# A four-layer hybrid decoder trunk on one core: masks, small weights and zeroed rows of a layer move to a pool of their own that is filled one stage earlier

## The chip, the core and the metric

The kernel runs on one core of one Trainium2 chip. The metric is the device time of one execution in microseconds (us), lower is better. TensorE (PE) multiplies matrices into PSUM, VectorE (DVE) and ScalarE (ACT) do the elementwise work, GpSimd (POOL) only fills tiles with constants here, and SyncE (SP) issues every DMA. Each engine works through its own instructions strictly in order; where one waits, everything behind it on that engine waits too.

## The reference

The trunk has 272 positions (16 learned meta tokens in front of 256 tokens) of width 1024 and four layers. Layer *i* has one token mixer of three kinds in turn, then a dense SwiGLU feed-forward block (FFN) with inner width 2816:

```python
for i in range(DEPTH):                      # 4 layers: fox, gla, gdn, fox
    y = rmsnorm(h, norm_mix[i])
    mix = (fox_mixer, gla_mixer, gdn_mixer)[i % 3](y, ...)
    h = h + mix
    h = h + swiglu(rmsnorm(h, norm_ffn[i]), w_gate_up[i], w_down[i])
return h[:, N_META:]
```

Fox is softmax attention with a forget bias, 16 heads of 64; GLA is gated linear attention with four heads; GDN is a gated delta rule with eight heads of 128 in chunks, whose inner step is a triangular solve:

```python
b = cumsum(g)                               # per chunk and head
lower = (k*beta) @ k.T * exp(where(strict, b_t - b_s, -inf))
u, w = triangular_solve(eye + lower, [v*beta, k*beta*exp(b)])
o = (q @ k.T * exp(where(incl, b_t - b_s, -inf))) @ (u - w @ state) + (q*exp(b)) @ state
```

All arithmetic is float32 in the reference.

## The kernel before

**Layout.** The residual `h` lies transposed in SBUF as eight tiles of 128 channels by 272 positions. Every dense product is kept near float32 precision by splitting both operands into a high and a low part (`zh`/`zl`, `oh`/`ol`, `ah`/`al` for the three kinds of activations, `wh`/`wl` for weights), so that a block of 128 x 128 weights against 272 columns costs three matmuls: high by high, high by low, low by high. I call such three matmuls a **block**, and name it by its operand: a `zh` block belongs to an input projection, an `oh` block to the mixer's output projection, an `ah` block to the FFN's second product. Chunked mixers work in three position tiles of 96, 96 and 80 (`TILES`).

**Weights.** 420 units of 512 KB, each eight blocks, arrive through one DMA each (`w`, issued by SP in `make_unit`, line 553 on). ACT copies a unit to `wh`, DVE subtracts to get `wl`. There are three raw buffers and three buffers of split units: the load of unit *u* waits until DVE has split unit *u*-3, and the split of *u* waits until PE is done with *u*-3. I count units from 0 in the order of the program: Fox 0 to 40, its FFN 41 to 106, GLA 107 to 139 with its output projection in the last eight, its FFN 140 to 205, GDN 206 to 246, and so on.

**Order of the work.** Nothing is scheduled on the chip. A planner in Python (`Trunk.turn`, `step`, `Lane.slot`, `Trunk.load`) runs generators for each small chain, and keeps for each engine a model of when it will be free and when each tile will be ready; dense blocks are the filler between the steps of the chains. PE's order is the planner's, and DVE, ACT, POOL and SP are ordered by the times that it computed. A load enters the model through `Trunk.load` (it moves the planner's clock of SP and of the DMA on), so a load that is moved or dropped also changes, by small amounts, the times by which the planner decides what stands next to what.

**Layers and their pools.** `run` (line 1720 on) calls, for each layer, `fox`, `gla` or `gdn` and then `ffn`. Each of these opens its own SBUF pools and closes them at its end, so the pools of a mixer lie on addresses that the FFN in front of it used; what is written first into them has to wait until the FFN's last reader, PE's last `ah` matmuls, is done. At the start of a mixer these are:

- `fox`: a load of its mask (`fmask`), used when the attention scores leave PSUM.
- `gla`: loads of its masks (`gmask`), of a tile of ones with zeros at the chunk starts (`rst`, 576 KB), by which one scan restarts its running sum at each chunk, and of a small weight (`wa`). `rst` and `wa` are used when the gate is computed.
- `gdn` (lines 1283 to 1296): loads of half masks (`half`) and a triangular mask (`tri`), two DVE casts of `tri` to `mask`, a cast of the identity to `eye`, a load of `rst`, and two tiles that DVE fills with zeros (`bs`, `brs`; `rows_tile` multiplies a column by 0).

**The seam between a mixer and its FFN, or an FFN and the next mixer.** For each of the eight output tiles *k*, DVE adds the product to the residual (`h<-h,ps`), ACT scales it to `zh` and squares it into `nsq`, DVE makes `zl` and adds the square to `nacc`. PE can run the next input projection for tiles 0 to 6 while tile 7 is still in this chain. After tile 7 PE sums `nacc` over the channels (`nacc,con`), DVE takes that as `ms` and computes the inverse root `rs` (nine instructions named `rq`), without which no projection can leave PSUM.

**GDN inside.** From `rs` a chain leads over the gate (`be`, `ax`, `l1p`), one scan (`b<-rst,ax`, line 1324), `rr` and `rc` to the decay matrices `d`. Later comes the inverse of the chunks' triangular matrices: a long DVE chain, then the merges (`xm,l`, `ym,xt`, `xt,ym`), then one solve for each of eight heads (`vb,xt`, `vn,l`, `d,vn`), beside the last input projections for q and v with their convolutions (`xc`, `yc`) on DVE. Four solved heads make a group; a group's sum of squares goes through the same inverse root, is spread by PE (`nacc,sel`) and gives four of the eight `oh` tiles, so that `oh` blocks of the first group can fill the gaps of the last solves.

## Time and profile before

| | us |
|---|---|
| median of three runs (lowest, highest) | 1561.16 (1558.8, 1566.98) |
| the profiled execution: its own time | 1560.21 |
| its span, first to last instruction | 1558.4 |
| PE busy / PE weight loads busy | 1498.1 / 1453.9 |
| DVE busy / ACT busy / POOL busy | 1096.2 / 780.2 / 17.1 |
| mean granted TensorE clock | 0.981 of full speed |
| moved by DMA | 225.85 MB, mean 145 GB/s |

Times of the trace count from the start of the span; the 1.8 us between span and time lie around it. In the profile a row of the timeline gives start, duration, engine, line, operation, `out<-in`, and in brackets how long the engine was idle before it and what ended that. Line 404 is the helper that issues every matmul, line 245 the one that issues every DVE, ACT and POOL instruction, line 377 the one for loads, so work is told apart by the names of its tiles. In the rows by window each engine has its busy time and its count of instructions; the column after them is the granted TensorE clock as a share of full speed.

The last residual tile of each stage is added at: first Fox layer 200 us, its FFN 398, GLA 541, its FFN 746, GDN 991, its FFN 1191, last Fox layer 1369; the last FFN runs to the end.

### The profile page before, as it was taken

The page shows a single profiled execution, that of the slowest core. Times are in us where ns is not written, and L with a number is a line of the kernel's source. Part 1 is how long each engine was busy: PE and PEld are TensorE (multiplying, and loading weights), DVE is VectorE, ACT ScalarE, POOL GpSimd, SP SyncE. Part 2 cuts the span into 40 slices and gives each one's busy share as a digit, 9 for nine tenths or more (in the row PEclk, how much of TensorE's full clock was granted, in tenths as well). Part 3 has the DMA queues.
Part 4 walks back from the last instruction along what each step waited for, and adds up shares of the span by engine and source line. Part 5 has one row for each costly group of instructions (what it writes and reads, how often), then busy time and mean ns, then how long its engine had stood idle before and what let it go on. Part 6 is the DMA issues. An engine that isn't in the chain of part 4 may idle for free.

```text
span 1558.4 us, 29526 instructions
## 1 busy us (share of the span) xinstructions
PE 1498.1 (96%) x11985; PEld 1453.9 (93%) x11985; DVE 1096.2 (70%) x2159; ACT 780.2 (50%) x1417; POOL 17.1 (1%) x56
## 2 busy tenths in 40 slices
PE   8899999999999999999897998999999999999999
PEld 7788999999999999999886897999999888999999
DVE  7778676665896776655779667866656777786653
ACT  5556554444455544444564544544445555654442
POOL 0000000000000000000200000000000000000000
PEclk9999999999999999999898898999999999999999
DMA  5232455555433455555333111555555333455564
GB/s 191 91 114 95 151 183 171 175 177 177 152 109 98 147 176 176 176 176 176 111 115 103 42 52 57 163 187 173 172 182 172 108 102 117 136 188 187 183 200 138
DMA packets 63897, 225.85 MB, mean 145 GB/s; under 512 B 7256, under 2 KB 9664, under 8 KB 63760
## 3 DMA queue, kind: packets, MB, share of 16 engines
q1 hardware_dynamic: 63760, 223.96, 43.9%
q8 instruction: 94, 1.54, 0.4%
q14 instruction: 43, 0.35, 0.1%
HBM read 222.88 MB, written 1.05 MB: 144 GB/s over the span
## 4 chain that ended last, share of the span: by engine, by line
PE 78%; DVE 9%; ACT 6%; issue 5%; DMA 0%; SPq 0%; POOL 0%; DVEq 0%; ACTq 0%; POOLq 0%
PE ps L404 78%; DVE wl L245 2%; ACT pr L245 2%; ACT wh L245 2%; DVE rq L245 1%; DVE pr L245 1%; DVE sm L245 1%; PE ps L409 1%; ACT d L245 1%; ACT pts L245 0%; DVE ri L245 0%; DVE raw L245 0%; DMA h<-in_h_dram 0%; DVE tmp L245 0%; DVE l1p L245 0%
## 5 line engine op out<-in xcount | busy, mean ns | idle before, releaser
L404 PE MATMUL ps<-zh,wh 128*128 128x272 f32 (+1 forms) x2400 | 712.1, 297 | 11.6 <-ACT zh L245 9.2
L404 PE MATMUL ps<-zh,wl 128*128 128x272 f32 (+1 forms) x2400 | 695.5, 290 | 5.4 <-DVE wl L245 5.4
L404 PE MATMUL ps<-zl,wh 128*128 128x272 f32 (+1 forms) x2400 | 696.6, 290 | 0.0
L245 ACT ACTIVATE wh<-w 128x1024 fp32r<-128x1024 f32 x420 | 443.6, 1056 | 392.5 <-PE ps L404 195.3
L245 DVE TENSOR_TENSOR wl<-w,wh 128x1024 fp32r<-128x1024 f32 x420 | 512.1, 1221 | 164.0 <-ACT wh L245 163.9
L404 PEld LDWEIGHTS ps<-zh,wh 128*128 128x128 f32 x2400 | 458.2, 191 | 21.4 <-ACT zh L245 9.5
L404 PEld LDWEIGHTS ps<-zh,wl 128*128 128x128 f32 x2400 | 458.3, 191 | 8.9 <-DVE wl L245 7.2
L404 PEld LDWEIGHTS ps<-zl,wh 128*128 128x128 f32 x2400 | 457.8, 191 | 0.2
L404 PE MATMUL ps<-al,wh 128*128 128x272 f32 (+1 forms) x704 | 202.0, 287 | 0.0
L404 PE MATMUL ps<-ah,wl 128*128 128x272 f32 (+1 forms) x704 | 201.3, 286 | 0.0
L404 PE MATMUL ps<-ah,wh 128*128 128x272 f32 (+1 forms) x704 | 200.7, 285 | 0.0
L404 PEld LDWEIGHTS ps<-ah,wh 128*128 128x128 f32 x704 | 133.0, 189 | 0.0
L404 PEld LDWEIGHTS ps<-al,wh 128*128 128x128 f32 x704 | 132.4, 188 | 0.0
L404 PEld LDWEIGHTS ps<-ah,wl 128*128 128x128 f32 x704 | 132.2, 188 | 0.0
L245 DVE TENSOR_TENSOR al<-a,ah 128x272 fp32r<-128x272 f32 (+1 forms) x88 | 38.6, 438 | 64.9 <-ACT ah L245 64.8
L245 DVE TENSOR_TENSOR s<-t,rs 128x272 f32<-128x272 f32 (+1 forms) x88 | 38.5, 437 | 64.5 <-ACT t L245 64.5
L404 PE MATMUL ps<-oh,wh 128*128 128x272 f32 (+1 forms) x256 | 76.3, 298 | 1.6 <-ACT wh L245 1.2
L404 PE MATMUL ps<-oh,wl 128*128 128x272 f32 (+1 forms) x256 | 75.4, 294 | 0.9 <-DVE wl L245 0.9
L404 PE MATMUL ps<-ol,wh 128*128 128x272 f32 (+1 forms) x256 | 75.1, 293 | 0.0
L245 ACT ACTIVATE zh<-h,par 128x272 fp32r<-128x272 f32 x64 | 32.7, 519 | 71.4 <-DVE h L245 70.6
L245 ACT ACTIVATE ah<-a 128x272 fp32r<-128x272 f32 (+1 forms) x88 | 36.8, 418 | 62.6 <-DVE a L245 62.6
L245 ACT ACTIVATE pr<-sm,mn 96x192 f32<-96x192 f32 (+3 forms) x96 | 42.2, 441 | 26.6 <-DVE mn L245 26.5
(224 smaller groups left out, 1501.5 us busy)
## 6 DMA issues: line engine op xcount, KB each, us to landing
w<-in_w_dram SPq DMA_DIRECT2D x420, 512.0 KB, 3.3
h<-in_h_dram SPq DMA_DIRECT2D x4, 272.0 KB, 5.4
out_dram<-h SPq DMA_DIRECT2D x8, 128.0 KB, 2.8
rst<-in_rst_dram SPq DMA_DIRECT2D x1, 576.0 KB, 6.0
mask<-in_fmask_dram SPq DMA_DIRECT2D x2, 210.0 KB, 5.6
con<-in_con_dram SPq DMA_DIRECT2D x1, 207.5 KB
mask<-in_gmask_dram SPq DMA_DIRECT2D x1, 126.0 KB, 3.1
par<-in_par_dram SPq DMA_DIRECT2D x1, 87.5 KB, 3.2
```

The source lines that it names most:

```text
L245: r = f(*args, **kw)
L404: ins = self.nc.tensor.matmul(out, lhsT, rhs, start=start, stop=stop)
L409: ins = self.nc.tensor.transpose(out, in_, self.con("ident")[:n, :n])
```

## The change

A new function `ready` opens a pool of its own for the next layer's mask, small weight, casts and zeroed tiles, loads or computes them, and leaves them in `self.pre`. `run` calls it for the first layer before the loop, and for every further layer right after the mixer in front of it is done and before that layer's FFN; the pool of the layer just ended is closed first. The mixers take their tiles from `self.pre`. `tri` lands in one of the two buffers that also hold the squares of the norm (`nsq`). Two tiles of ones and zeros are no longer loaded: GLA's `rst` is filled by two POOL memsets, and GDN's scan is split into one for each position tile, with a broadcast column of ones in the place of `rst`.

```diff
+    def ready(self, kind, last):
+        cx = ExitStack()
+        pp = cx.enter_context(self.tc.tile_pool(name="pre" + kind, bufs=1))
+        v = self.v
+        if kind == "fox":
+            w = sum(t0 + n for t0, n in TILES)
+            mask = pp.tile([96, w], F32, tag="mask", name="mask")
+            self.load(mask, self.io["fmask"][:, (w if last else 0) : (2 * w if last else w)])
+            self.pre = mask
+        elif kind == "gla":
+            mask = pp.tile([96, 96 + 5 * 48], F32, tag="mask", name="mask")
+            self.load(mask, self.io["gmask"])
+            wa = pp.tile([16, 512], F32, tag="wa", name="wa")
+            self.load(wa, self.io["wa"])
+            self.pre = mask, wa
+        else:
+            half = pp.tile([96, 96], F32, tag="half", name="half")
+            self.load(half, self.io["dmask"][:, 96:192])
+            tri = self.zp.tile([128, T], F32, tag="nsq", name="tri", bufs=2)[:96, :96]
+            self.load(tri, self.io["dmask"][:, 0:96])
+            dmask = pp.tile([96, 176], F32R, tag="mask", name="mask")
+            v.tensor_copy(dmask[:, 0:96], tri)
+            v.tensor_copy(dmask[:, 96:176], tri[:, 0:80])
+            eye = pp.tile([96, 96], F32R, tag="eye", name="eye")
+            v.tensor_copy(eye, self.con("ident")[:96, :96])
+            bs = self.rows_tile(pp, "bs")
+            brs = self.rows_tile(pp, "brs", T, 128)
+            self.pre = half, dmask, eye, bs, brs
+        return cx
...
@@ gla
-            self.load(rst, self.io["rst"])
-            wa = cp.tile([16, 512], F32, tag="wa", name="wa")
-            self.load(wa, self.io["wa"])
+            g.memset(rst, 1.0)
+            g.memset(rst.rearrange("p (i c) -> p i c", c=96)[:, :, 0:1], 0.0)
...
@@ gdn
-            half_mask = gp.tile([96, 96], F32, tag="half", name="half")
-            self.load(half_mask, self.io["dmask"][:, 96:192])
...
+            half_mask, dmask, eye, bs, brs = self.pre
...
-                v.tensor_tensor_scan(b, rst, x, 0.0, ALU.mult, ALU.add)
+                one = self.con("strip")[:8, 142:143]
+                for t0, n in TILES:
+                    v.tensor_tensor_scan(b[:, t0 : t0 + n], one.to_broadcast([8, n]), x[:, t0 : t0 + n], 0.0, ALU.mult, ALU.add)
...
@@ run
+            pre = self.ready(self.layers[0][1][0], n == 1)
             for i, (li, (kind, j)) in enumerate(self.layers):
...
                 getattr(self, kind)(j, lo, f"g_ffn{li}")
+                pre.close()
+                if not last:
+                    pre = self.ready(self.layers[i + 1][1][0], i == n - 2)
                 self.ffn(lo, None if last else f"g_mix{self.layers[i + 1][0]}", last)
```

Three places show what moves; a row's `x2` means that it stands twice.

DVE before, at the seam from GLA's FFN to GDN (`wl` is the split of a weight unit, the rest as above):

```order
L245 TENSOR_TENSOR wl<-w,wh 128x1024 x2
L245 CAST mask<-tri 96x96
L245 CAST mask<-tri 96x80
L245 CAST eye<-con 96x96
L245 TENSOR_SCALAR bs<-con 128x272
L245 TENSOR_SCALAR brs<-con 128x272
L245 TENSOR_TENSOR h<-h,ps 128x272
L245 SCALAR_TENSOR_TENSOR zl<-h,par,zh 128x272
```

The same place after the change; the `h` is tile 7, the last of the seam:

```order
L245 TENSOR_TENSOR wl<-w,wh 128x1024 x2
L245 TENSOR_TENSOR h<-h,ps 128x272
L245 SCALAR_TENSOR_TENSOR zl<-h,par,zh 128x272
L245 TENSOR_TENSOR nacc<-nacc,nsq 128x272
L245 TENSOR_SCALAR nacc<-con 128x272
L245 TENSOR_TENSOR wl<-w,wh 128x1024
```

The five instructions in front of tile 7 are gone from there. On ACT, tile 7's `zh` and `nsq` also come one `wh` copy earlier, and on PE `nacc,con` comes after seven `zh` blocks where it came after nine.

DVE after the change at the seam from GLA to its FFN, 200 us earlier in the program; before, the two casts are not there and the rest is the same. The `h` in the second row is tile 6, the last one tile 7:

```order
L245 TENSOR_TENSOR wl<-w,wh 128x1024
L245 TENSOR_TENSOR h<-h,ps 128x272
L245 SCALAR_TENSOR_TENSOR zl<-h,par,zh 128x272
L245 TENSOR_TENSOR nacc<-nacc,nsq 128x272
L245 CAST mask<-tri 96x96
L245 CAST mask<-tri 96x80
L245 TENSOR_TENSOR wl<-w,wh 128x1024
L245 TENSOR_TENSOR h<-h,ps 128x272
```

The first `wl` is that of unit 140, the second that of unit 141. `eye`, `bs` and `brs` stand some 30 rows further ahead, in GLA's last steps, between an `ob` and the `ol` of head tile 5. On SP the load of `half` comes after unit 137 and that of `tri` after unit 143; before, both came after unit 210. The masks of GLA and of the last Fox layer move ahead in the same way, to after unit 44 and after unit 235.

The planner also set GDN's second half anew. PE before, where the last input projection passes over into the output projection, among the last solves:

```order
L404 MATMUL ps<-vb,xt 96x128
L404 MATMUL ps<-zh,wh 128x272
L404 MATMUL ps<-zh,wl 128x272
L404 MATMUL ps<-zl,wh 128x272
L404 MATMUL ps<-oh,wh 128x272
L404 MATMUL ps<-oh,wl 128x272
L404 MATMUL ps<-ol,wh 128x272
```

PE after the change, from the last `zh` block to the first `oh` block:

```order
L404 MATMUL ps<-nacc,sel 128x272
L404 MATMUL ps<-vb,xt 96x128 x2
L404 MATMUL ps<-vn,l_8812 80x128 x4
L409 MATMUL ps<-con,vt 96x128 x2
L409 MATMUL ps<-con,vt 80x128
L404 MATMUL ps<-nacc,sel 128x272 x3
L404 MATMUL ps<-vb,xt 96x128
L404 MATMUL ps<-vb,xt 80x128 x2
L404 MATMUL ps<-vn,l_8812 96x128
```

The spreading of the first group's root (`nacc,sel`) has moved from before the last nine `zh` blocks to behind them, so no block stands between the last `zh` and the first `oh` any more; seven `oh` blocks then follow in one piece. On DVE the first group's `og` products, which came ahead of the last two convolutions, now come behind them. Further ahead in the merges, four `zh` blocks have left one gap and are spread over later ones. The number of blocks is the same.

More of the change, by code (lines that the diff above doesn't have):

```diff
@@ L781, in fox @@
             tp = cx.enter_context(self.tc.tile_pool(name="foxt", bufs=2))
-            mask = cp.tile([96, w], F32, tag="mask", name="mask")
-            self.load(mask, self.io["fmask"][:, (w if lo else 0) : (2 * w if lo else w)])
+            mask = self.pre
             qg = cp.tile([128, 1], F32, tag="qg", name="qg")
@@ L990, in gla @@
             lp = cx1.enter_context(self.tc.tile_pool(name="glal", bufs=2))
-            mask = cp.tile([96, 96 + 5 * 48], F32, tag="mask", name="mask")
-            self.load(mask, self.io["gmask"])
+            mask, wa = self.pre
             rst = lp.tile([128, W], F32, tag="qe", name="rst")
-            self.load(rst, self.io["rst"])
-            wa = cp.tile([16, 512], F32, tag="wa", name="wa")
-            self.load(wa, self.io["wa"])
+            g.memset(rst, 1.0)
+            g.memset(rst.rearrange("p (i c) -> p i c", c=96)[:, :, 0:1], 0.0)
             mi = mask.bitcast(I32)
@@ L1282, in gdn @@
             gp = cx1.enter_context(self.tc.tile_pool(name="gdng", bufs=1))
-            half_mask = gp.tile([96, 96], F32, tag="half", name="half")
-            self.load(half_mask, self.io["dmask"][:, 96:192])
-            tri = tp.tile([128, T], F32, tag="sq", name="tri", bufs=4)[:96, :96]
-            self.load(tri, self.io["dmask"][:, 0:96])
-            dmask = gp.tile([96, 176], F32R, tag="mask", name="mask")
-            v.tensor_copy(dmask[:, 0:96], tri)
-            v.tensor_copy(dmask[:, 96:176], tri[:, 0:80])
-            eye = gp.tile([96, 96], F32R, tag="eye", name="eye")
-            v.tensor_copy(eye, ident[:96, :96])
-            rst = tp.tile([128, T], F32, tag="sq", name="rst", bufs=4)[:8]
-            self.load(rst, self.io["rst"][:8, :T])
-            bs = self.rows_tile(gp, "bs")
+            half_mask, dmask, eye, bs, brs = self.pre
             be = gp.tile([128, T], F32, tag="be", name="be")
-            brs = self.rows_tile(gp, "brs", T, 128)
             rc = gp.tile([96, 3, 128], F32, tag="rc", name="rc")
```

## The prediction

> **What bounds the kernel now.** I read the page first: the busy line and the chain of work that ended last.
>
> ```profile
> PE 1498.1 (96%) x11985; PEld 1453.9 (93%) x11985; DVE 1096.2 (70%) x2159; ACT 780.2 (50%) x1417; POOL 17.1 (1%) x56
> PE 78%; DVE 9%; ACT 6%; issue 5%; DMA 0%; SPq 0%; POOL 0%; DVEq 0%; ACTq 0%; POOLq 0%
> ```
>
> PE is busy 1498 of 1558 us. A change that removes no matmul can win only from the 60 us in which PE stands, and from slow matmuls behind such stands. So I took the busy times by window, to see where PE stands.
>
> ```profile
> 180.00:400.00 220.00, 220.00 (x1749) 219.92 (x1748) 144.90 (x216) 105.16 (x150) 1.87 (x2) 1.00 0.54 179
> 740.00:745.00 5.00, 3.73 (x30) 3.51 (x28) 1.04 (x5) 1.07 (x1) 4.22 (x8) 1.00 0.40 129
> 745.00:750.00 5.00, 3.10 (x11) 2.77 (x12) 4.35 (x10) 2.71 (x4) 3.81 (x10) 0.56 0.03 10
> 765.00:770.00 5.00, 2.25 (x18) 2.05 (x17) 4.62 (x14) 1.47 (x2) 0.00 (x0) 0.95 0.61 192
> 785.00:790.00 5.00, 2.86 (x21) 2.42 (x19) 2.40 (x4) 4.98 (x15) 0.10 (x1) 1.00 0.33 107
> 945.00:950.00 5.00, 4.63 (x33) 3.89 (x31) 4.77 (x11) 3.97 (x12) 0.00 (x0) 1.00 0.00 0
> 960.00:965.00 5.00, 1.30 (x7) 0.72 (x5) 3.18 (x8) 0.69 (x2) 0.00 (x0) 0.91 0.00 0
> ```
>
> The first row lies in the first FFN, with PE (the second number) busy throughout: what the change puts or removes there costs and wins nothing. The second and third are the entry of GDN: 3.2 us of standing and a clock of 0.56. Then the waits: of the constants that the change touches, one alone is ever waited for after 560 us, beside weights.
>
> ```profile
> ACT wh L245 <- DMA w<-in_w_dram: 4.9, 3, 1.8
> DVE mask L245 <- DMA tri<-in_dmask_dram: 4.0, 1, 4.0
> ```
>
> The timeline at that wait, by engine (start, duration, and in brackets the idle time before):
>
> ```profile
> 738.86 1.22 DVE L245 TENSOR_TENSOR wl<-w,wh 128x1024 fp32r<-128x1024 f32 x1 [1.37 <-ACT wh L245]
> 740.76 0.33 POOL L245 MEMSET rr<- 128x272 f32 x1 [269.21 <-PE ps L404]
> 741.15 0.42 SPq L377 DMA_DIRECT2D tri<-in_dmask_dram  x1
> 743.44 0.29 PE L404 MATMUL ps<-zl,wh 128*128 128x272 f32 x1
> 744.05 0.75 DVE L245 CAST mask<-tri 96x96 fp32r<-96x96 f32 x2 [3.96 <-DMA tri<-in_dmask_dram]
> 744.72 0.19 DVE L245 CAST eye<-con 96x96 fp32r<-96x96 f32 x1
> 744.84 0.28 DVE L245 TENSOR_SCALAR bs<-con 128x272 fp32r<-128x272 f32 x1
> 745.05 0.91 DVE L245 TENSOR_SCALAR brs<-con 128x272 fp32r<-128x272 f32 x1
> 745.88 0.42 DVE L245 TENSOR_TENSOR h<-h,ps 128x272 f32<-128x272 f32 x1
> 746.90 0.59 PE L404 MATMUL ps<-zh,wh 128*128 128x272 f32 x1 [3.17 <-ACT zh L245]
> ```
>
> DVE is free at 740.08, but its next instruction is the cast of `tri`, whose load could start only when the FFN released the address. Behind the cast stands the residual's last tile, on that `zh`, and on `zh` PE, which ran out of blocks at 743.73.
>
> **The change part by part.**
>
> *Entry of GDN.* With the five instructions gone, `h` waits only for the FFN's last matmul. POOL, which waits for the same, started at 740.76; so `h` starts at 740.8, 5.1 us earlier. `zh` follows about 1.0 us after it (745.88 to 746.90), ready at 741.8, before PE runs out: the 3.17 us go. PE also loses time behind the stand:
>
> ```profile
> 751.58 0.43 PE L404 MATMUL ps<-zh,wh 128*128 128x272 f32 x1
> 751.81 0.43 PE L404 MATMUL ps<-zh,wl 128*128 128x272 f32 x1
> 752.61 0.29 PE L404 MATMUL ps<-zl,wh 128*128 128x272 f32 x1
> 752.74 0.30 PE L404 MATMUL ps<-zh,wh 128*128 128x272 f32 x1
> ```
>
> Until 752.3 matmuls start 0.23 us apart, afterwards 0.13. Some 20 matmuls from 746.9 on lose 0.1 us each, another 2 us, so PE alone would be 5.2 earlier. What PE meets next is the standing at 765 to 770, where it waits for the chain from `ms` over `rs` and the scan. That chain starts behind `h` on DVE: 5.1 earlier, less the 0.3 or so that PE still takes until it can sum. I take **-5.0**. Bounds: -3.2 (only the standing comes back), -5.8 (DVE's whole delay, 740.08 to 745.88). The later standings of GDN end with the same chain and move with it.
>
> The Trainium skill (TensorE: Matmul & The Clock Gate, Part 1: The HAM clock gate) has the clock halved only by an idle window of about 3.4 us, and given back by a busy one. Taken strictly, a stand of 3.17 us need not halve it, and the term would be -3.2 if the slow stretch came from something else. The trace's rows show the half rate right behind the stand, so I keep it.
>
> *The scan in three pieces.* It stands on that chain.
>
> ```profile
> L245 DVE TENSOR_TENSOR_SCAN b<-rst,qe x1: 2548/2548/2548, 433.8 to 433.8; 128x1152 f32<-128x1152 f32 x1
> L245 DVE TENSOR_TENSOR_SCAN b<-rst,ax x1: 714/714/714, 765.1 to 765.1; 8x272 f32<-8x272 f32 x1
> ```
>
> (2548 - 714) / 880 columns is 2.08 ns a column and 0.15 us fixed; three scans make 3 x 0.15 + 272 x 0.00208 = 1.0 us instead of 0.71: **+0.3**, bounds +0.1 and +0.6.
>
> *`eye`, `bs`, `brs` at the end of GLA.* They stand there on DVE between two steps that make the last `ol` tiles. The 0.91 us of `brs` falls while POOL fills tiles; the same instruction elsewhere:
>
> ```profile
> L245 DVE TENSOR_SCALAR nacc<-con x3: 290/301/583, 400.0 to 749.1; 128x272 fp32r<-128x272 f32 x3
> ```
>
> Without POOL I take 0.29, so three cost 0.19 + 0.28 + 0.29 = 0.76 us of DVE. No quoted row says how much slack PE has behind the last `ol`; between nothing and the whole I take less than half: **+0.3**, bounds 0 and +0.8. (The Trainium skill, SBUF — State Buffer, Who interferes with whom, says why: casts and this operation can hold the port pair that DVE shares with GpSimd, and one then blocks the other fully. By its rule alone the fills would cost nothing extra at the new place; no POOL row stands there in the trace.)
>
> *The casts of `tri` at the seam from GLA to its FFN.* Here the change adds a wait: DVE comes to the cast after tile 6, and behind it stand the split of unit 141 and tile 7. On SP `tri` follows the load of unit 143, which waits for the split of unit 140.
>
> ```profile
> 536.91 1.22 DVE L245 TENSOR_TENSOR wl<-w,wh 128x1024 fp32r<-128x1024 f32 x1
> 538.18 0.33 SPq L377 DMA_DIRECT2D w<-in_w_dram  x1
> 539.58 0.43 DVE L245 TENSOR_TENSOR nacc<-nacc,nsq 128x272 f32<-128x272 f32 x1
> 540.43 0.29 PE L404 MATMUL ps<-zh,wh 128*128 128x272 f32 x1
> 541.07 0.43 DVE L245 TENSOR_TENSOR h<-h,ps 128x272 f32<-128x272 f32 x1
> 544.98 0.62 PE L404 MATMUL ps<-nacc,con 128*128 128x272 f32 x2
> tri<-in_dmask_dram SPq DMA_DIRECT2D x1, 36.0 KB, 2.8
> DMA to landing us min/median/max: 3.1/3.4/7.9
> ```
>
> The rows are `wl` of unit 140, the load of unit 143, the end of tile 6, PE's first FFN block, tile 7, and PE's sum; the last two are landings, of `tri` and of the mask tiles. `tri` would be issued at 538.6 and land 2.8 us later, at 541.4. DVE reaches the cast at 540.0: it waits 1.4, casts for 0.4, ends the split of unit 141 (1.22) at about 543.1, and tile 7 comes about 1.9 late. PE has seven blocks of unit 140 at 0.38 us, so it first needs unit 141 at 540.43 + 2.65 = 543.1, and the sum at 545.0 now has 2 us of slack behind tile 7's `nacc`. Both covers are just used up: **+0.4**, bounds 0 and +2.0.
>
> *The rest, nothing.* GLA's masks and `wa`, and the last Fox mask, were never waited for; GLA's 576 KB of `rst` and the two new POOL memsets lie in stretches like the first window row, with PE busy to the full. If that cover were gone, a memset of that size would cost about 1 us: POOL's 1.87 us in that row are two.
>
> *The new order in GDN's second half.* Same blocks, other gaps. The `oh` blocks of the first group run between these rows before:
>
> ```profile
> 944.27 0.29 PE L404 MATMUL ps<-oh,wh 128*128 128x272 f32 x1
> 946.53 1.57 DVE L245 SCALAR_TENSOR_TENSOR yc<-xc,par,yc 128x272 f32<-128x272 f32 x3
> 948.02 1.22 DVE L245 TENSOR_TENSOR wl<-w,wh 128x1024 fp32r<-128x1024 f32 x1
> 958.66 0.29 PE L404 MATMUL ps<-ol,wh 128*128 128x272 f32 x1
> ```
>
> Now they wait until DVE is through both convolutions and a split (the second convolution is as long as the first: 1.57 + 1.22 + 1.57, 4.4 us) and the first `og`. PE has about 20 small matmuls meanwhile, at 0.14 us (33 instructions in 4.63 us in the window row at 945) some 3 us, so it may stand 1 to 2 us. Against that the last convolutions no longer stand behind four `og` and `ol` instructions, and the last solve, on which the standing at 960 hangs, starts sooner. Nothing in the trace shows this order; I take **+1.0**, bounds -2 (half of the standing at 960 goes) and +4 (both standings of the window rows at 945 and 960, 0.4 + 3.7, once more).
>
> Sum: -5.0 + 0.3 + 0.3 + 0.4 + 1.0 = -3.0. On the profiled execution's 1560.2 that makes 1557.2, on the median of the three runs (1561.2) 1558.2; I forecast 1557.7.
>
> **The rivals.**
>
> *The gain is swallowed in GDN.* The chain after 765 us could be held by ACT (4.98 of 5 us busy in the row at 785) or the new order could give back its 4 us. Against the first: ACT's queue there also starts with the chain. Result: 1560 to 1562, no change.
>
> *Slower: the wait for `tri` at the new seam.* If `tri`, queued behind 512 KB of weights, lands like the slowest mask (7.9 us after 538.6, at 546.5), the split of unit 141 ends at 548.1, PE stands 5 us and then runs about 2 us slow: 7 instead of 0.4, result about 1564. It makes the kernel slower than before from a stand of about 1.5 us on (1.5 + 2 slow against 3.4 left), that is from a landing about 4.3 us after the issue. Against it: DMA engines are busy only half the time beside an FFN (0.54 in the first window row), and `tri` itself took 2.8.
>
> *More gain.* The entry gives 5.8, the seam hides, and the new order wins 2: 1553.
>
> **How the numbers follow.** Forecast 0.60 (1555.5 to 1560), swallowed 0.14, slower 0.12 (1562 to 1567, by the seam or by the bound of the new order), more gain 0.14 (1550 to 1555). The range is 1551 to 1564. A change of 0.5%, 7.8 us, is about what a measurement of this kernel can tell from none. Faster than 1553.4 is the better half of the last case: 0.10. Slower than 1569 needs two bounds at once: 0.04. The rest, 0.86.
>
> **What would show it.** Right: no `tri` wait at 740, `h` about 0.7 us after DVE's last split, PE without a gap there and at full clock, 765 to 770 still with a standing of like size but 5 us earlier; at 540 a wait of DVE of 1 to 2 us with little standing of PE. Wrong: a standing of PE over 2 us at 543, the scans over 1.3 us, or the distance from the scan to GDN's last `oh` block longer by over 3 us than before.

## The result, and the profile after

| | before | after |
|---|---|---|
| median on one chip (lowest, highest; runs) | 1558.8 (1551.68, 1566.98; 13) | 1572.3 (1566.95, 1578.67; 13) |
| profiled execution: its own time / span | 1560.21 / 1558.4 | 1568.21 / 1566.4 |

After takes 1.0082 times as long as before, 95% interval 1.0063 to 1.01: some 13 us slower. The forecast was 1557.7 us, with 1551 to 1564 as its range. That lies above the range, in the part that got a chance of 0.04 (slower than 1569). First the page's busy line and the chain of work that ended last, after the change.

```profile
PE 1502.2 (96%) x11985; PEld 1453.9 (93%) x11985; DVE 1096.8 (70%) x2161; ACT 779.5 (50%) x1417; POOL 18.1 (1%) x58
PE 81%; DVE 11%; ACT 5%; issue 1%; DMA 1%; SPq 0%; DVEq 0%; ACTq 0%
```

PE's instructions are the same 11985, but the span grew by 8.0 us, and PE is counted busy for 4.1 of them: the same matmuls took longer. Where, is best read by cutting the program at the rows `ms<-ps` that end each stage. Stage lengths in us, from ms row to ms row (the first from the start of the span, the last to its end), of the two profiled executions:

| | Fox | FFN | GLA | FFN | GDN | FFN | Fox | FFN |
|---|---|---|---|---|---|---|---|---|
| before | 203.0 | 198.6 | 144.0 | 203.7 | 246.2 | 199.4 | 178.1 | 185.5 |
| after | 198.0 | 199.2 | 143.4 | 199.1 | 265.0 | 198.2 | 178.2 | 185.3 |

Two stages got clearly shorter and one much longer. The first Fox layer's 5.0 are not the change's: PE's order there is the same, but before ran at half clock from 158.5 to 165.3 us and after did not. Another run of before's own program up to GDN (e13, below), without that half clock, took 198.2 there. GLA's FFN, which ends with the entry of GDN, won 4.6. GDN lost 18.8, although the part of it up to the scan won 1.1 more (ms to scan 15.74 before, 14.67 after). From the scan to the stage's end it takes 250.3 where it took 230.4: **19.9 us longer**. The prediction named as a sign of failure that the distance from the scan to GDN's last `oh` block grows by over 3 us; it went from 225.7 to 244.5.

The entry first, in DVE's timeline of after: tile 7's `h`, a zero fill, the sum `ms` and the three scans.

```profile
735.57 0.44 DVE L245 TENSOR_TENSOR h<-h,ps 128x272 f32<-128x272 f32 x1 [0.65 <-PE ps L404]
739.01 0.83 DVE L245 TENSOR_SCALAR nacc<-con 128x272 fp32r<-128x272 f32 x1
739.76 0.42 DVE L245 TENSOR_SCALAR ms<-ps 128x272 f32<-128x272 f32 x1
754.43 0.81 DVE L245 TENSOR_TENSOR_SCAN b<-con,ax 8x96 f32<-8x96 f32 x3
```

`h` waits for PE alone, no longer for `tri`. Then busy times by window, to set beside the rows of before: the seam at GLA's end, the entry, the standing that follows it, and two windows of GDN's last solves. After the window's length come the busy times of PE, PE's weight loads, DVE, ACT and POOL, then the granted clock, the DMA share and GB/s.

```profile
535.00:540.00 5.00, 4.85 (x38) 4.59 (x37) 3.05 (x7) 1.95 (x4) 0.00 (x0) 1.00 0.31 105
735.00:740.00 5.00, 5.00 (x41) 4.92 (x40) 3.81 (x7) 2.70 (x4) 4.39 (x8) 1.00 0.34 116
755.00:760.00 5.00, 2.39 (x11) 2.39 (x12) 3.81 (x14) 0.70 (x2) 0.00 (x0) 0.69 0.46 170
945.00:950.00 5.00, 3.44 (x23) 2.45 (x22) 4.56 (x14) 2.85 (x8) 0.00 (x0) 1.00 0.31 105
950.00:955.00 5.00, 3.53 (x25) 2.63 (x23) 4.43 (x10) 2.33 (x7) 0.00 (x0) 1.00 0.36 107
```

At the entry PE is busy throughout at full clock, where before it stood 3.2 us and ran at 0.56. At 945 to 955, PE stands 3.0 of 10 us: that is new. The 19.9 us come apart at two more PE rows, the last `zh` block and the first `oh` block. PE's timeline of after from the one to the other, of which the rows with standing and the spreading of the root are shown:

```profile
945.63 0.29 PE L404 MATMUL ps<-zl,wh 128*128 128x272 f32 x1
946.50 0.46 PE L404 MATMUL ps<-vn,l 96*96 96x128 f32 x2 [0.36 <-ACT vn L245]
947.59 0.39 PE L404 MATMUL ps<-nacc,sel 128*128 128x272 f32 x1 [0.64 <-DVE nacc L245]
948.80 0.46 PE L404 MATMUL ps<-vb,xt 96*96 96x128 f32 x2 [0.43 <-DVE vb L245]
950.97 0.53 PE L409 MATMUL ps<-con,vt 128*96 128x128 f32 x3 [0.48 <-ACT vt L245]
953.32 0.67 PE L404 MATMUL ps<-vb,xt 80*80 80x128 f32 x4 [0.91 <-DVE vb L245]
954.35 0.37 PE L404 MATMUL ps<-oh,wh 128*128 128x272 f32 x1
```

For 8.7 us PE has only small matmuls: 30 of the solves and the four `nacc,sel`, in groups that wait for a DVE or ACT step. Before, the blocks never ran out; the first `oh`, at 944.27, follows the last `zl`:

```profile
944.15 0.28 PE L404 MATMUL ps<-zl,wh 128*128 128x272 f32 x1
```

The other half lies further ahead, in the merges. Windows of 10 us there, of after:

```profile
860.00:870.00 10.00, 10.00 (x94) 8.45 (x92) 4.66 (x13) 4.00 (x10) 0.20 (x2) 0.50 0.15 53
870.00:880.00 10.00, 10.00 (x54) 7.89 (x53) 4.08 (x14) 0.37 (x1) 0.00 (x0) 0.68 0.01 2
900.00:910.00 10.00, 10.00 (x70) 8.57 (x69) 4.13 (x9) 2.81 (x6) 0.10 (x1) 0.51 0.08 24
```

And of before, whose merges begin 9.8 us later (765.1 + 90.8 against 754.4 + 91.7):

```profile
870.00:880.00 10.00, 10.00 (x108) 8.75 (x107) 4.76 (x12) 3.94 (x10) 0.20 (x2) 0.73 0.16 55
880.00:890.00 10.00, 9.63 (x76) 8.06 (x76) 7.61 (x20) 4.95 (x15) 0.10 (x1) 1.00 0.05 11
910.00:920.00 10.00, 10.00 (x100) 9.09 (x99) 7.38 (x18) 3.54 (x8) 0.10 (x1) 1.00 0.01 2
```

PE counts as busy for 9.63 to 10.00 of 10 in all six rows, but for most of the time at half clock in after: the busy time hides the loss. Half clock held in after from 859.3 for 17.1 us and from 900.3 for 13.7 us; in before from 868.5 for 6.8 us, and not a second time.

The Trainium skill (TensorE: Matmul & The Clock Gate, Part 1: The HAM clock gate) gives half clock after an idle window of about 3.4 us. By that rule, read with the profile's busy time, windows in which PE is busy 10.00 of 10 keep their clock; these rows do not agree.

### The profile page after: what moved, and what is told of

The parts are those of the page before. It is cut to its first block, busy times and chain, and to the rows that moved or that the text cites. A ratio compares the mean times of both kernels' runs of the same rounds, so it can differ in the third digit from the quotient of the medians.

```text
span 1566.4 us, 29529 instructions
## 1 busy us (share of the span) xinstructions
PE 1502.2 (96%) x11985; PEld 1453.9 (93%) x11985; DVE 1096.8 (70%) x2161; ACT 779.5 (50%) x1417; POOL 18.1 (1%) x58
## 4 chain that ended last, share of the span: by engine, by line
PE 81%; DVE 11%; ACT 5%; issue 1%; DMA 1%; SPq 0%; DVEq 0%; ACTq 0%
PE ps L404 80%; DVE wl L245 3%; ACT wh L245 1%; ACT pr L245 1%; DVE rq L245 1%; DVE pr L245 1%; DVE sm L245 1%; PE ps L409 1%; ACT d L245 1%; DMA w<-in_w_dram 1%; DVE yc L245 1%; ACT pts L245 0%; DVE ri L245 0%; DVE d L245 0%; DMA h<-in_h_dram 0%
## 5 line engine op out<-in xcount | busy, mean ns | idle before, releaser
L404 PE MATMUL ps<-ah,wh 128*128 128x272 f32 (+1 forms) x704 | 201.0, 285 | 0.0
L245 ACT ACTIVATE pr<-sm,mn 96x192 f32<-96x192 f32 (+3 forms) x96 | 42.2, 441 | 26.3 <-DVE mn L245 26.2
```

The costliest lines, as they stand in the source:

```text
L245: r = f(*args, **kw)
L404: ins = self.nc.tensor.matmul(out, lhsT, rhs, start=start, stop=stop)
```

## The experiments

A term used below: the planner's **books** are its own model of when engines and tiles are free. A moved instruction changes the chip and the books; the kernels below separate the two. **Old order** and **new order** mean PE's order in GDN as in before and as in after. Every ratio is to the kernel before, run beside it on the same chip. The table gathers what the first readings rest on: us from the scan to three PE or DVE rows, the clock lost up to the last `zh` (PE's busy time in 1-us windows times one minus the granted clock), and PE's standing from there to `ms`.

| kernel | last `zh` | first `oh` | `ms` | clock lost | standing |
|---|---|---|---|---|---|
| before (old order) | 179.1 | 179.2 | 230.4 | 9.6 | 6.8 |
| e1 (old) | 183.1 | 183.2 | 233.3 | 13.0 | 6.8 |
| e5 (old) | 190.9 | 191.0 | 240.9 | 22.0 | 6.8 |
| e12 (old) | 190.8 | 190.9 | 242.2 | 22.1 | 6.8 |
| after (new order) | 191.2 | 199.9 | 250.3 | 21.6 | 10.2 |
| e2 (new) | 191.2 | 201.1 | 251.2 | 22.0 | 10.1 |
| e8 (new) | 182.3 | 191.0 | 239.1 | 12.4 | 7.8 |
| e13 (old merges, late spreading) | 178.6 | 182.7 | 232.8 | 9.6 | 8.0 |
| e9 (new, extra matmuls) | 186.4 | 195.1 | 244.0 | 6.7 | 4.9 |
| e11 (old, extra matmuls) | 181.7 | 181.8 | 231.2 | 3.4 | 2.6 |

**Moves and order apart.** e1 makes all the moves of the change, but keeps before's books, so the order stays the old one (an excerpt; `quiet` takes an instruction out of the books, `book` and `book_load` write one in):

```diff
-                    pre = self.ready(self.layers[i + 1][1][0], i == n - 2)
+                    with self.quiet():
+                        pre = self.ready(self.layers[i + 1][1][0], i == n - 2)
...
             half_mask, dmask, eye, bs, brs = self.pre
+            self.touch(half_mask, self.book_load(96 * 96), True)
+            at = self.book_load(96 * 96)
+            self.touch(dmask[:, 0:96], self.book(v, 96, at), True)
...
```

> All moves of the change are kept (masks, casts and zeroed tiles in pools of their own, one stage earlier, no tiles of ones loaded, three scans), but the planner's books are kept as before the change, so that PE, ACT and all DVE work that wasn't moved stand in the order of before. Order theory (the new order in GDN's second half leaves stretches of small matmuls, in which the granted clock falls to half for 17.1 and 13.7 us; that costs about 10 us, and the last gaps another 6): without the new order only the gain at GDN's entry is left, about 5 us under the kernel before: 1554 (1551 to 1557), and from the scan to GDN's last residual tile as long as before, 226 us. Queue theory (the last Fox mask's load, now in SP's queue behind unit 235, waits 34 us for its address and holds up the weights of GDN's last units): the load stands there here too, so the time stays at 1570 to 1574, and that distance at 243.

Measured: 1556.48 us, ratio 0.9984 (0.9964 to 1.0003). The moves alone do no harm, and bring no gain clear of noise. Their gain is smaller than foretold: GLA's FFN and the entry together take 202.74 + 14.52 = 217.3 us against 203.69 + 15.74 = 219.4. The timeline of e1, DVE and POOL behind tile 7, tells why:

```profile
741.17 0.44 DVE L245 TENSOR_TENSOR h<-h,ps 128x272 f32<-128x272 f32 x1 [0.65 <-PE ps L404]
744.40 2.09 POOL L245 MEMSET xm<- 96x768 f32 x3
744.63 4.41 DVE L245 TENSOR_SCALAR nacc<-con 128x272 fp32r<-128x272 f32 x2
746.42 2.10 POOL L245 MEMSET xt<- 96x768 f32 x3
748.96 0.43 DVE L245 TENSOR_SCALAR ms<-ps 128x272 f32<-128x272 f32 x1
```

A zero fill of `nacc`, 0.29 us elsewhere, begins beside POOL's six fills and ends only when those are over; `ms` comes behind it. In before DVE was late itself, and the fill met only the end of POOL's run. The Trainium skill (SBUF — State Buffer, Who interferes with whom) says that the engine which issues second is blocked fully while the first holds the shared port pair; the row agrees that DVE is blocked, and shows that it lasts over both groups of fills (2.09 + 2.10 us), not for one instruction.

e2 is the reverse: before's instructions where they were, with the books of after, so that the order is the new one.

```diff
+                if not last:
+                    self.book_ready(self.layers[i + 1][1][0])
...
-            self.load(mask, self.io["gmask"])
+            with self.quiet():
+                self.load(mask, self.io["gmask"])
...
+            self.touch(mask, self.at[0], True)
```

> The reverse: loads, casts, zeroed tiles and the single scan stand where they stood before the change, but the planner's books are those of the changed kernel, so that PE and ACT have exactly its order. Order theory: the loss of the changed kernel without its gain at GDN's entry: 1577 (1573 to 1581), 14 to 22 us over the kernel before. Queue theory: no early load of the mask, so no loss: 1556 to 1562.

Measured: 1574.33 us, ratio 1.0097 (1.0071 to 1.0123), scan to `ms` 251.2. The order alone carries the whole loss.

**A rival: the moved mask load blocks SP.** After loads the last Fox mask ahead of time, and SP's waits from 860 us on hold a long one for it, for the address to come free:

```profile
SPq L377 <- DVE ym L245: 33.6, 1, 33.6
```

e3 is after with this load back in its old place, and its entry left in the books.

```diff
-            self.load(mask, self.io["fmask"][:, (w if last else 0) : (2 * w if last else w)])
+            if last:
+                self.touch(mask, self.book_load(96 * w), True)
+            else:
+                self.load(mask, self.io["fmask"][:, 0:w])
```

> The changed kernel with one thing put back: the last Fox mask is loaded when that layer starts, behind GDN's FFN, so that nothing stands between the weight units 235 and 236 on SP; every engine's order is otherwise that of the changed kernel. Order theory: same as the changed kernel, 1572 (1569 to 1575). Queue theory: 10 us or more come back: 1556 to 1562.

Measured: 1573.41 us, ratio 1.0088 (1.0062 to 1.0115), scan to `ms` 251.2. The wait costs nothing that these runs could tell; this rival falls.

**Is it the clock in the merges?** e4 is after with one dense matmul more ahead of the small ones in each bank of the merges (36 in all). Each writes a bank that the real matmuls overwrite, so nothing of the computation is left out, here and in all kernels below with extra matmuls.

```diff
                 p = yield from self.bank()
+                self.fill(p, z[0][0])
```

> The changed kernel with 36 more matmuls of full size (128 x 128 on 272 columns): one ahead of each group of small matmuls in the six merges, written to the bank that the group then overwrites. The rest of the order stays. They cost 36 x 0.125 = 4.5 us of PE at full clock if none falls into a gap. Clock theory (PE's use of its array in a 3.41 us window of the clock falls to 0.40 and less in the merges, and then the clock is halved until a window has about 0.8): the windows stay over 0.45, the half-clock stretches of 17 and 14 us shrink to a third, and 10 us come back for 3 to 4.5: 1565 (1561 to 1569). If the order costs time by its waits and not by the clock: 1574 to 1577.

Measured: 1571.28 us, ratio 1.0087 (1.0055 to 1.0119). The first stretch at half clock in the merges stayed at 20.5 us as in e2 and e3, the second fell from 13.7 to 3.4. This lies between the two expectations. The granted clock of its runs was 0.980 on the mean, where after's runs had 0.977, but the 36 matmuls cost 36 x 0.126 = 4.5 us of PE, and nothing was left of the gain.

**The zero fill mended.** e5 is e1 with the `nacc` fill taken behind `ms`; the books are unchanged.

```diff
+        with self.quiet(self.now):
+            ys = self.rows_tile(self.zp, "nacc", bufs=2)
         yield from self.rsqrt(self.zp, y, mm)
-        ys = self.rows_tile(self.zp, "nacc", bufs=2)
```

> The first experiment (all moves, old order) with the two zeroed tiles of GDN's output norm (nacc, two DVE instructions of 0.29 us elsewhere) filled where they are used and no more at GDN's entry, where in the first, third and fourth experiment one of them lasted 4.2 to 4.4 us beside POOL's fills of xm and xt, in front of ms. Theory of the entry: that one instruction ate the gain; without it ms and all behind it come 3.5 us earlier, from the previous stage's ms to the scan 213.7 us instead of 217.3, and the time is 1553 (1550 to 1556). Rival: the entry is held by PE or the chain behind ms anyway: distance 216 to 217, time 1556 to 1558.

Measured: 1559.15 us, ratio 0.9995 (0.9968 to 1.0022). The entry did what was foretold (198.79 + 14.69 = 213.5 us, 5.9 less than before), and yet nothing came of it: in the same old order the merges ran at half clock for 23.9 + 10.2 us instead of 6.8, and lost 12.4 us of clock more up to the last `zh`. I had not expected that an earlier start alone can do that.

e6 is the same fill in after, with the new order.

> The changed kernel with the same late zero fill. Theory of the entry: 0 to 3.5 us under the changed kernel's 1572.3 (its own profiled run had an instruction of only 0.83 us there, the other kernels with its entry 4.4): 1569.5 (1567 to 1572), and in the profile a distance of 213.7 from ms to the scan. Rival: no difference, 1572 to 1574. The loss in GDN's second half stays in either case: 250 us from the scan to the next ms.

Measured: 1570.72 us, ratio 1.0063 (1.0045 to 1.0081). Its one profile, of an execution of 2906 us, isn't read; the ratio leaves that execution out. The time stays with the new order.

e7 is e5 with two extra matmuls in each merge bank of the first group (36 in all).

```diff
                 p = yield from self.bank()
+                for _ in range(2 * (1 - grp)):
+                    self.fill(p, z[0][0])
```

> The fifth experiment with two more full-size matmuls ahead of each of the 18 groups of small ones in the first three merges, whose output the group overwrites. Clock theory: windows of 3.41 us in which PE streams under 0.37 of the columns that it could halve the clock for the next one; in the first merges of the old order they hold 0.24 to 0.38, and 6.8 to 13.7 us of half clock follow. Two more matmuls a group (0.028 of a window each, 5 to 8 groups a window) bring them over 0.45: that stretch goes, 3.4 to 6.8 us back for 36 x 0.125 = 4.5 us of work, of which a part falls into gaps: -1 (-4 to +1.5) against the fifth. If the small matmuls cost by their waits and not by the clock: +3.5 to +4.5.

Measured: 1557.39 us (1551.79 to 1561.73), ratio 0.9986 (0.9969 to 1.0003). After 850.5 us the merges hold full clock. The same window in e5:

```profile
870.00:880.00 10.00, 10.00 (x82) 8.13 (x83) 2.38 (x7) 2.55 (x7) 0.10 (x1) 0.50 0.14 48
```

and in e7:

```profile
860.00:870.00 10.00, 10.00 (x116) 8.49 (x115) 4.16 (x11) 3.61 (x9) 0.20 (x2) 1.00 0.17 54
870.00:880.00 10.00, 9.64 (x72) 7.64 (x70) 7.25 (x20) 3.11 (x7) 0.10 (x1) 1.00 0.00 1
```

Scan to `ms` fell from 240.9 to 231.4 us. In the medians the gain over e5 is 1.8 us only: e5's own runs spread over 20 us (1548 to 1568), so its profiled one was an unlucky one. What the extra matmuls buy is mostly a narrower spread.

**How little it takes.** e8 is before with nothing moved; one DVE entry that is never issued stands in the books at GDN's entry.

```diff
             gp = cx1.enter_context(self.tc.tile_pool(name="gdng", bufs=1))
+            self.book(v, T)
```

> The kernel before with one thing changed: at GDN's start the planner books one more DVE instruction of 0.24 us that is never issued. No instruction is added, removed or changed, only the order that the planner then writes differs, and comes out much like that of the changed kernel (the four blocks leave the merges). Order theory: the loss without any of the moves: 1573 (1567 to 1578). If the loss needs the moves: 1560 (1557 to 1563).

Measured: 1572.78 us, ratio 1.0077 (1.0055 to 1.01). One number in the planner's model, and no change to the work, costs as much as the whole change. The order in GDN is the new kind: the last `zl` of e8 at 944.94, the first `oh` at 953.62. Its profiled run was a mild one in the merges (12.4 us of clock lost), so here the tail shows by itself.

**The order with the clock held.** Three kernels get extra matmuls wherever GDN stands long: 20 ahead of `rr`, 78 ahead of the first merge, two a bank in the first group's merges, 36 ahead of the last output group. e9 is after with these (and one a bank in the second group), e10 before, e11 the moves in the old order with the late fill.

```diff
+                for _ in range(0 if grp or i3 else 78):
+                    self.fill(p, z[0][0])
                 for i in range(4):
                     self.mm(p[:n, i * n : i * n + n], u[:, i], xmn[:, i])
...
+            for _ in range(36 if len(tiles) == 4 and i == 4 else 0):
+                self.fill(p, self.old_z)
             self.mm(p[:, :T], self.pick(slice(0, 128), row(i)), ys)
```

> The changed kernel with 188 more full-size matmuls, whose output is overwritten, that keep PE streaming where it stands or trickles: 20 in the standing ahead of the transposes of rr, 78 in the standing of 11.4 us behind the inverse, 36 in that of 5.2 us ahead of the last nacc,sel, and two (first three merges) or one (last three) ahead of each group of small matmuls. The first three lots fit into the standings (2.5, 9.8 and 4.5 us); the 54 in the merges cost at most 54 x 0.125 = 6.8 us. Clock theory: of the 24.7 to 29.8 us that half clock costs in GDN with this order, some 18 go: 1572 - 18 + 6.8 = 1561 (1557 to 1565). If the order costs by its waits: 1576 to 1579.

> The kernel before with the same matmuls in the same standings and two ahead of each group in the first three merges (170). Clock theory: its half clock in GDN costs 12.9 to 15 us, of which 8 to 10 go, for 36 x 0.125 = 4.5 us: 1560 - 9 + 4.5 = 1555 (1552 to 1559); and since the clock no longer falls in either order, the distance to the changed kernel so padded shrinks from 13 us to 6 or less. If the waits count: 1563 to 1565.

> All moves, the order of before, the late zero fill (fifth experiment), two matmuls ahead of each group in the first three merges (seventh) and the same matmuls in the three standings: a version that should beat both kernels. Against the seventh (1557.4; its profile has half clock over 758 to 762, 840 to 850 and 956 to 963, of which 1.7 + 1.9 + 1.9 us are lost): 1552 (1549 to 1555). If the standings' clock doesn't matter, because what follows waits on other engines: 1557.

Measured: e9 1567.85 us, ratio 1.0056 (1.003 to 1.0081); e10 1561.27, ratio 1.0023 (1.0009 to 1.0036); e11 1556.96, ratio 0.9989 (0.997 to 1.0007). All three lie above what the clock theory expected (1565, 1559 and 1555 at most). Three things follow. Holding the clock gave after some 4.5 us back on balance, not most of its loss. For before it costs a little more than it gives, and e11 came out as its rival said, no faster than e7. And between the medians of e9 and e11, which both make the moves, 10.9 us remain. Of these, 18 x 0.126 = 2.3 are the 18 matmuls that e9 has more. A small part is clock, for e9 doesn't hold it in every run: its runs go from 1558.89 us at 0.996 to 1574.66 at 0.984, those of e11 lie at 0.988 to 0.997. At 0.993, e9 took 1563.82 (one run) and e11 1553.88 and 1554.35; 9.7 less 2.3 leaves 7.4 for the order at the same clock. PE's timeline of e9 at the last `zh` and the first `oh`:

```profile
942.69 0.29 PE L404 MATMUL ps<-zl,wh 128*128 128x272 f32 x1
951.42 0.37 PE L404 MATMUL ps<-oh,wh 128*128 128x272 f32 x1
```

and of e11:

```profile
939.87 0.28 PE L404 MATMUL ps<-zl,wh 128*128 128x272 f32 x1
939.99 0.29 PE L404 MATMUL ps<-oh,wh 128*128 128x272 f32 x1
```

From the last `zh` to `ms` e9 takes 57.6 us and e11 49.5: 8.1 longer, with the clock lost under 2 us in both. The solves that the old order sets between `zh` blocks stand alone in the new one: up to the first `oh`, 30 of their matmuls without a block in after, none in before.

**Which of the two places?** e12 is after, with the planner made to take four `zh` blocks at the one gap in the merges where it had declined them; from there on the order becomes the old one by itself.

```diff
-        if not self.warm and self.step(soon):
+        if (not self.warm or 6172 <= self.npe < 6184) and self.step(soon):
```

> The changed kernel with its own books and one decision of the planner forced: at the 6172nd matmul of PE, in the first merges, it takes four zh blocks, as the planner did before the change. From there on it decides for itself, and writes the order of before again, matmul for matmul, to the end of GDN (the second half's tail with the late og included). Order theory: the whole loss hangs on that one decision; 1557 (1554 to 1561), as the first experiment with its 1556.5. If the loss came from a move itself (loads, pools, casts): 1570 to 1574.

Measured: 1561.97 us, ratio 1.0021 (0.9999 to 1.0044), 1 us above its range. After's ratio was 1.0082: some 10 us of the loss are gone by the place of four blocks. Its `oh` blocks follow the `zh` blocks at once again:

```profile
950.95 0.28 PE L404 MATMUL ps<-zl,wh 128*128 128x272 f32 x1
951.07 0.29 PE L404 MATMUL ps<-oh,wh 128*128 128x272 f32 x1
```

In its profiled run the merges still lost 22.1 us of clock, as after's did, so what came back there is the tail: 51.5 us from the last `zh` to `ms`, where after took 59.1.

e13 is before with the spreading of the first group's root held until no projection is left, as in after; the merges are before's.

```diff
                 yield s_ev[grp]
+                while not grp and (self.bg or self.open):
+                    yield 0.1
```

> The kernel before with one wait in the planner's code: the first group's output norm may start only when no projection block is left, as it came out in the changed kernel. PE's order differs from that of before only from there on (6544th matmul; the merges stay), and stands like that of the changed kernel: nacc,sel behind the last zh, no block between the last zh and the first oh, og behind the last two convolutions. If the tail is the other part of the order's cost (8.7 to 10 us pass between the last zh and the first oh in every profile with the new order, 0.1 with the old; 1 to 2 us come back behind): 1559 + 7 = 1566 (1563 to 1569). If the whole cost is the half clock in the merges: 1558 to 1561.

Measured: 1559.83 us, ratio 1.0004 (0.9988 to 1.002), against the expectation of 7 us more. The late spreading by itself costs 54.2 - 51.3 = 2.9 us in the tail. The median doesn't show it because these runs had more clock, 0.9824 on the mean against 0.9811 in the runs of before beside them: at 0.984, four runs of e13 took 1559.7 us on the mean, and five of before (beside all the experiments) 1555.2. The gap without a block is 4.1 us there and 8.7 to 10 in the new order: it holds 15 matmuls of solves in e13 and 30 in after, so in after more solves are still to be done when the projections run out.

e14 is after with the last input projection kept back until the root is spread, to fill the gap.

```diff
+            self.holding = self.bg[-1:]
...
-        ev = d.evs[k]
+        ev = Ev() if d in self.holding else d.evs[k]
```

> The changed kernel whose planner holds the last projection back until the first group's output tiles are made, so that a few zh blocks are left for the solves; PE's order differs from that of the changed kernel only from the 6519th matmul on, in the tail, while DVE and ACT keep theirs (og behind the last convolutions). If the tail costs because PE has no block to fill it: 1572 - 3 = 1569 (1566 to 1571). If it costs because DVE comes to og late, or if all of the loss lies in the merges: 1571 to 1574.

Measured: 1570.74 us, ratio 1.0084 (1.0065 to 1.0102). 9.6 us without a block remain (191.4 to 201.0 after the scan), and nothing comes back. But by tile and shape its rows stand in after's order on every engine: no block came into the gap. So this run does not tell what filling the gap would win.

## Why the prediction was wrong

**Step 1, the entry (-5.0): right.** GLA's FFN and ms to scan together went from 219.4 to 199.11 + 14.67 = 213.8, 5.7 less, near the outer bound of -5.8; e5 and e11 give 5.9. What I hadn't seen is that tile 7, once earlier, lets the `nacc` fill run into POOL's fills, which eats 3 to 4 us in e1 (2.2 won in all). In after's profile the fill met one POOL fill only and took 0.83 instead of 0.29. That neighbourhood belonged to the row that I used for `brs`, and I did not ask it of the other fills.

**Step 2, the scans (+0.3): the lower bound.** Three took 0.81 where one took 0.71.

**Steps 3 and 4, the seam (+0.7 together): right.** DVE's timeline of after there:

```profile
536.35 0.32 DVE L245 CAST mask<-tri 96x96 fp32r<-96x96 f32 x2 [1.79 <-DMA tri<-in_dmask_dram]
537.73 0.42 DVE L245 TENSOR_TENSOR h<-h,ps 128x272 f32<-128x272 f32 x1
540.65 0.43 DVE L245 TENSOR_SCALAR ms<-ps 128x272 f32<-128x272 f32 x1
```

DVE waits 1.79 (1.4 foretold). PE, in the window row at 535, stands 0.15 us and keeps its clock. GLA takes 142.9 to 144.8 us with the moves and 142.4 to 144.0 without; where both ran at half clock for 3.4 us about 523, the difference is 0.5 to 0.8. So the rival of a late `tri` did not come.

**Step 5, the rest (0): right,** down to a mask load that held SP for 33.6 us without cost (e3).

**Step 6, "Same blocks, other gaps", +1.0, bounds -2 and +4: this failed.** It measured +19.9 in the profile; in medians 14.3 and 12.4 for the new order without the moves (e2, e8). Over the whole way from the scan to `ms` the 19.9 are 11.8 of lost clock (24.7 against 12.9), 5.6 of standing (31.9 against 26.3) and 2.5 in which PE counts as busy. I priced the new order by standings of PE alone, and let "the number of blocks is the same" stand for the work being the same. Two terms are missing in it.

*The tail.* I gave PE "about 20 small matmuls" and 3 us between the last `zh` and the first `oh`, and 1 to 2 us of standing; it was 34 and 8.7 us, and PE stood 3.4 us longer up to `ms` (10.2 against 6.8). From the last `zh` to `ms` after takes 59.1 us and before 51.3, **+7.8**; what isn't standing is small matmuls that no block covers, and in part work that stood ahead of the last `zh` before. All profiles in the new order have 56.8 to 60.0 there, all in the old one 49.4 to 51.5. The late spreading makes 2.9 of it (e13); the rest comes only together with the blocks that left the merges' gap (e12 puts both back). The piece of the order in front of me said that no block stood between `zh` and `oh`; what it could not say is how long that lasts, and I should have counted the solves left behind the last block.

*The clock in the merges.* From the scan to the last `zh` after takes 12.1 us more, and 12.0 of them are clock (21.6 against 9.6 lost). I had taken clock losses for a matter of standings; here it halves with PE busy. I counted what PE streams in each window of 3.41 us of the clock records, in dense matmuls of 128 rows by 272 columns, other shapes by their columns and rows, f32 ones double, since their spacing is (27 is what fits at full rate, at 0.126 us each; `h`: the window ran at half clock). Before from 844.6 on, then after from 835.4 on:

```
before 0 0h 0h 8.8h 15.1h 13.1 6.7 6.8h 11.8h 16.4 14.6 28.2 21.4 17.2 14.6 17.7 19.6 13.1 14.0 15.3
after  0 0h 0h 10.9h 14.8h 11.4 7.2 8.4h 10.1h 7.8h 9.3h 12.5h 23.3 20.9 13.2 17.1 18.6 13.9 11.1 7.2h 10.7h 9.9h 12.7h 26.2
```

Below about 11 the next window runs at half clock, and from half clock it takes about 11 again to return. Over six traces, 2542 windows at full clock, this rule misses seven; it was drawn from these same traces, and of some 120 windows at half clock it misses about nine. At half clock those 11 are most of what PE can do, so merges with few blocks stay there: before's 11.8 returned, after's 10.1, 7.8 and 9.3 did not. The four `zh` blocks that left this gap are 12 matmuls, just the size of the threshold. But the old order fell as deep when it started at another place in the window (e5, e12), so in a single profile this part is luck of the start as well as the order.

**The rivals.** The gain was swallowed at the first rival's place, GDN's second half, but five times over. Nothing held the chain after 765 us: it moved with the entry, as foretold, and the merges begin 91.7 us after the scan where they began 90.8 after it.

**How the 13 us of the median split.** Every run lists its granted clock, and the time follows it. At a clock of 0.979 or 0.980, 33 runs of before took 1561.2 us on the mean, and five of after 1568.5: 7.3 are left at the same clock. I also laid straight lines of time against clock through the runs of all kernels, with one slope for all (265 runs; 1.28 us more for each 0.001 of clock less; the runs scatter by 1.5 us about the lines). At the same clock they put after 6.2 us over before, e2 6.3, e8 6.1, e13 2.6, e12 0.7, and e1 0.5 under it, each to within about 1. The rest is clock: 0.9766 on the mean of after's runs, 0.9817 on that of before's 114 runs beside the experiments, which makes 6.5 us at that slope. So the order costs about as much by what it does at the same clock as by the clock that it loses. And this loss isn't luck alone: the new order without extra matmuls has means of 0.975 to 0.978 (after, e2, e3, e6, e8, e14), the old one 0.980 to 0.983 (before, e1, e5, e12).

**What stays open.** Why the merges of the new order lose clock more often is argued from the count of one profile of each, not tested run by run; no run here sets where the windows lie. What a block in the tail's gap would win is not shown (e14). And no kernel here beats before clear of noise: e1, e7 and e11 are the best, 0.9984 (0.9964 to 1.0003), 0.9986 (0.9969 to 1.0003) and 0.9989 (0.997 to 1.0007).

## What to carry to other kernels

Where a planner writes the order, test an edit of the program twice: its moves with the old order, and the new order without its moves. The smallest entry in its model can cost more than the edit wins (e8), and "the same blocks" is no bound; count how long PE is without a block, and which chain is left for that time. Read the granted clock beside PE's busy time: a PE that is busy 10 of 10 can be at half speed on thin matmuls. And where the clock differs from run to run, compare runs at the same clock before a difference of medians is put down to an edit, or to nothing (e13).

## What the runs showed of the hardware

- Half clock comes in whole multiples of 3.41 us: 3.4, 6.8, 10.2, 13.7, 17.1, 20.5 and 23.9 in these traces. By the count above, which was drawn from these traces, it follows the columns streamed in a window (about 11 of 27 dense matmuls), not PE's busy time.
- The windows run free of the kernel: with the same order of PE, the same layer took 178.1 or 180.9 us (last Fox, before and e5), as a stretch of 6.8 us at half clock came or not.
- A DVE zero fill of 0.29 us that starts beside a run of POOL fills took 4.2 us (4.41 with its neighbour, e1) and ended when they did.
